# A decoder layer with 32 streamed experts: gathering four experts at once, first weights by column halves, the far branch moved to the end

## The chip, the cores and the metric

The kernel runs on one core of a Trainium2 chip. The metric is the device time of one execution in microseconds (us). Time before: 1111.27 us, the median of three runs (1111.09 to 1114.21).

## The reference, cut to what matters

One post-norm decoder layer on 256 tokens of width 1024, all in float32. After the attention part comes a mixture of 32 experts, of which each token takes four:

```python
x = layer_norm(ALPHA * x + mix, ln1_g, ln1_b)          # after attention
logits = x @ w_router + b_router
top_vals, top_idx = top_k(logits, 4)
gates = softmax(top_vals)
for each expert e, over the tokens that chose it:
    h = x @ w1[e] + b1[e]                               # 1024 -> 2048
    glu = minimum(h[..., 0::2], 7); lin = clip(h[..., 1::2], -7, 7)
    y = (glu * sigmoid(1.702 * glu) * (lin + 1)) @ w2[e] + b2[e]   # 1024 -> 1024
    moe += gate * y
out = layer_norm(ALPHA * x + moe, ln2_g, ln2_b)
```

The weights of all experts are read once: 32 x (8 + 4) MiB.

## The kernel before

**Stages.** Until about 143 us the kernel computes the attention part and the routing. From there on it goes through the 32 experts, one after the other, and ends with the second norm.

**The weight stream.** The list `stream` holds 384 blocks of 1 MiB, twelve for each expert: eight of w1, each 128 rows of all 2048 columns (one row of 8 KB in a partition), and four of w2, each 256 rows of 1024 columns (two rows of 4 KB in a partition). The last four blocks are w2 of expert 31 by column halves (rows of 2 KB, two DMAs a block). SyncE issues them in this order. There are NB = 23 places in on-chip memory (15 in `arena`, 8 named `later`), and block i goes to the place of block i - 23, so its DMA waits until all that reads block i - 23 is done. `load(n)` issues the blocks up to number n; where it stands in the program decides on which reader a block waits. An expert's first twelve places are therefore the last limit of the stream: while expert e - 1 holds its twelve, only blocks up to 12e + 10 are out.

**One expert on TensorE.** The class `Ordered` and the dictionary `last` keep each engine's instructions in the order in which the program writes them. For each expert TensorE does: four bias matmuls (`first_biases`, `ph<-b_s,sel`), 32 matmuls of the first product into the two halves of `ph` (for each of eight row blocks k both halves n, 64 token slots times two column groups side by side), the clamped SwiGLU on VectorE and ScalarE (`swiglu`), four transposes of its result (`turn_act`), 16 matmuls of the second product (`second`), and at every even expert the matmuls that add the pair before to the sums (`combine`). At every odd expert the next two experts' tokens are gathered (class `Pair`): four 128x512 matmuls with token rows as the result, a copy, eight transposes, eight scaled copies into `XG`. This work fills the wait for the SwiGLU.

**More than 64 tokens.** Experts 4 to 29 (`INLINE`) have a branch for 32 further slots (`more`), taken if the expert's count is above 64. In this data one expert takes it, expert 4. It stands behind the first matmul of the next expert, and only after it are the twelve places of the expert free (`load(e * NW + NB)` behind it). For experts 4 to 9 (`TWICE`) it is in two parts: `more_first` in the expert itself, after its first product, which frees the eight w1 places, and `more_second` in the next expert. All that is left (more than 64 tokens in experts 0 to 3, 30, 31, or more than 96) is in one far branch at expert `HOST` = 20, on TensorE, VectorE, ScalarE and SyncE, never taken here. Branches that are expected to be skipped have a hint on TensorE (`expect`); the far branch has none.

**Norm rows.** The residual ALPHA * (normed x * g + b) is added at experts 21 to 28 (`KEPT`), in eight pieces: `spread_cols` makes rows of g and b on TensorE (four 128x128 matmuls each), VectorE makes the piece, one matmul with the identity adds it. g2 and be2 of the second norm are made in the same way at expert 30.

Of the kernel before, what the change touches and what calls it, by code (L numbers as in the profile page):

```python
# [20 lines left out]
P = 128  # L21
# [23 lines left out]
TWICE = range(4, 10)  # L45
HOST = 20
KEPT = 21
MORE = ((64, 32), (96, 32), (128, 64), (192, 64))
@with_exitstack
def decoder_layer(ctx, tc, x, w_in, b_in, sinks, w_out, b_out, ln1_g, ln1_b, w_router, b_router,  # L50
# [26 lines left out]
    MW = 6016  # L77
# [350 lines left out]
    wl = w2[0, NE - 1].rearrange("(a m i p) f -> m p a i f", a=2, m=2, p=P)  # L428
# [184 lines left out]
    XG = V(M, KD, 2 * SLOTS)  # L613
    XTOK = V(M + 1024, 2, 512)
    OH = V(M + 2048, NT, 2 * SLOTS)
    GOH = V(M + 2304, NT, 192)
    GSB = [V(M + 2688 + i * S, S) for i in range(2)]
    Y = [V(M + 3200 + i * 512, 512) for i in range(2)]
    GLU, LIN, AT = (M + 4224 + i * 512 for i in range(3))
    KEEP = V(M + 5760, 2, P)  # L620
    xnT = V(M + 1024, KD, P)
    rt = GLU
    b2_sb = V(M + 3200, D)[0:NE]
    gT = V(M + 2688, S)[0:NE]
# [87 lines left out]
    class Pair:  # L712


        def __init__(self, e, px):
            self.e, self.px = e, px

        def choose(self, t):
            for i in range(2):
                chosen(OH[:, t, i * SLOTS:(i + 1) * SLOTS], self.e + i, t, 0, SLOTS)  # L720

        def tokens(self, t, ns=(0, 1)):
            for n in ns:
                pe.matmul(self.px[n], OH[:, t, :], xn[:, t, n * 512:(n + 1) * 512],
                          start=(t == 0), stop=(t == NT - 1))

        def copy(self):
            act.copy(XTOK[:, 0, :], self.px[0])
            dve.tensor_copy(XTOK[:, 1, :], self.px[1])

        def turn(self, pts):
            pts = [pt.rearrange("p (a b) -> p a b", a=4) for pt in pts]
            for n in range(2):
                for i in range(4):
                    pe.transpose(pts[n][:, i, :], XTOK[:, n, i * P:(i + 1) * P], ident)
            for i in range(4):
                for n in range(2):
                    affine(XG[:, n * 4 + i, :], pts[n][:, i, :], n * 4 + i, n)

# [4 lines left out]
    def first_biases(hs, e):  # L744
        for n in range(2):
            for j in range(2):
                first_bias(hs[n][j * 64:(j + 1) * 64, :], e, SLOTS, j * 1024 + n * 512)

    first = Pair(0, banks[2:4])
# [31 lines left out]
    first.tokens(0, (0,))  # L781
    norm(1, 0)
    route(1)
    first.tokens(0, (1,))
    first_biases([ph[:, n, :] for n in range(2)], 0)
# [3 lines left out]
    first.tokens(1)  # L789
    first.copy()  # L790
    first.turn(banks[0:2])
# [4 lines left out]
    def gather(e, off, w):  # L796
# [3 lines left out]
        xg, xtok = V(M + 1024, KD, SLOTS), V(M + 1024, D)[:, :wq]  # L800
# [25 lines left out]
    def turn_act(aT, i0, n, lin):  # L826

        pa = TP().rearrange("p (a b) -> p a b", a=4)
        for i in range(n):
            pe.transpose(pa[:, i, :], V(lin + i * P, P), ident)  # L830
        act.copy(aT[:, i0:i0 + n, :], pa[:, :n, :])

    def second(w2s, aT, swap=0, label=None):

        py = TP()
        for k in range(KD):
            if k == 2 and label:
                expect(label)
            for j in range(2):
                n = j ^ swap  # L840
                pe.matmul(py[j * 64:(j + 1) * 64, :], aT[:, k % 4, k // 4 * 64:(k // 4 + 1) * 64],
                          w2s[k // 2][:, k % 2, n * 512:(n + 1) * 512], start=(k == 0), stop=(k == KD - 1))
        return py
# [45 lines left out]
    def last_second(w2s, hs):  # L889

        aT = V(AT, 4, P)
        ys, py = (Y[1], V(GLU, 512)), (TP(), ph[:, 1, :])

# [5 lines left out]
        def turn(m):  # L899
            pa = ph[:, 1 - m, :].rearrange("p (a b) -> p a b", a=4)  # L900
            for i in range(2):
                pe.transpose(pa[:, i, :], V(LIN + m * 256 + i * P, P), ident)
            act.copy(aT[:, 2 * m:2 * m + 2, :], pa[:, :2, :])

# [4 lines left out]
        for m in range(2):  # L909
            swiglu(hs[m], 256, GLU + m * 256, LIN + m * 256, AT + m * 256)  # L910
            if m == 0:
                turn(0)
        step(0, 0, 0)
        turn(1)
        act.activation(small[:, 255:256], small[:, 255:256], AF.Sqrt)
        step(0, 0, 1)
# [12 lines left out]
    def over_first(e, b, w1v, xg, lin):  # L929
# [4 lines left out]
        for n in range(wq // 512):  # L934
# [3 lines left out]
            for k in range(KD):  # L938
                for j in range(nq):
                    c0 = j * wq + n * 512  # L940
                    pe.matmul(po[j * w:(j + 1) * w, :], xg[:, k, :w], w1v[k][:, c0:c0 + 512],
                              start=False, stop=(k == KD - 1))
            swiglu(po, 256, GLU + n * 256, lin + n * 256, M + 1536 + n * 256)
# [36 lines left out]
    def expect(label):  # L980

        with tc.issue_after(last[pe].ins):
            tc.mark_branch_hint_location(label, "LikelyTaken", [EN.PE])
# [8 lines left out]
    def more(e, c, w1s, w2s, b=0, deep=False, label=None):  # L992

        off, w = MORE[b]
        with behind(c, off, label):
            w1v = w1s() if callable(w1s) else w1s
            xg = gather(e, off, w)
            over_weights(e, b)
            n = over_first(e, b, w1v, xg, LIN)
            gsb = over_rows(b)  # L1000
            aT = V(M + 1536, 4, P)
            turn_act(aT, 0, n, LIN)
# [3 lines left out]

    def more_first(e, c, w1s):

        with behind(c, MORE[0][0], f"first{e}"):
            n = over_first(e, 0, w1s, gather(e, *MORE[0]), GLU + 256)  # L1010
            turn_act(KEEP, 0, n, GLU + 256)

    def more_second(e, c, w2s):

# [92 lines left out]
    for e in range(NE):  # L1107
# [5 lines left out]
        if e == NE - 1:  # L1113
            hs[1] = TP()
            TP.places = [TP()]
# [182 lines left out]
```

## Time and profile before

| | before |
|---|---|
| median of three runs | 1111.27 us |
| the profiled execution | 1111.0 us |
| its span in the trace | 1109.3 us |
| mean granted clock of TensorE | 0.989 |
| bytes moved | 423.70 MB, mean 382 GB/s |
| TensorE busy | 1039.1 us (94%) |
| VectorE, ScalarE busy | 283.9 us, 181.8 us |
| SyncE's DMA queue | 94.6% of sixteen engines' span |

The page divides the span into 40 slices of 27.7 us; a TensorE that waits for weights inside a run of pipelined matmuls still counts as busy there, so the bytes per slice say more than the busy share. The views by stretch give the mean rate of all DMA traffic in a stretch (last column). 1 MiB is 1.0486 MB, so at r GB/s a block takes 1048.6 / r us.

### The profile page before, as it was taken

How to read it: one execution, taken by the hardware profiler on the slowest of the kernel's cores; microseconds unless marked ns; L12 is line 12 of the kernel's file. 1: busy time of each engine (PE TensorE's matmuls, PEld its weight loads, DVE VectorE, ACT ScalarE, POOL GpSimd, SP SyncE). 2: the span in 40 equal slices, each digit the busy share in tenths (PEclk: the TensorE clock that was granted, in tenths of full speed). 3: DMA queues.
4: the chain of work that ended last, by engine and by line, in shares of the span. 5: the costliest groups of instructions: out<-in, count | busy, mean ns of one | idle time of the engine just before them, and what ended most of it. 6: DMA issues, size and time to landing. Idle time of an engine off the chain costs nothing. (4 is left out here: it accounts for less than half of the span.)

```text
span 1109.3 us, 11948 instructions
## 1 busy us (share of the span) xinstructions
PE 1039.1 (94%) x4634; PEld 417.4 (38%) x4634; DVE 283.9 (26%) x687; ACT 181.8 (16%) x374; POOL 7.1 (1%) x20
## 2 busy tenths in 40 slices
PE   8789899999899999999999999979999999899995
PEld 7465433333233333333333333323333333333431
DVE  6666532121221212121212121211222121221114
ACT  5434421011010101010101010100101010011102
POOL 0000000000000000000000000000000000000001
PEclk9999999999999999999999999999999999899998
DMA  9978599998978999999999999989999999999993
GB/s 331 283 296 328 222 371 416 417 417 326 409 299 347 417 415 417 408 419 417 418 417 417 416 417 414 416 326 387 416 417 417 415 416 416 416 416 415 417 413 121
DMA packets 85952, 423.70 MB, mean 382 GB/s; under 512 B 8256, under 2 KB 15200, under 8 KB 52992
## 3 DMA queue, kind: packets, MB, share of 16 engines
q1 hardware_dynamic: 85568, 422.02, 94.6%
q8 instruction: 65, 1.06, 0.4%
q10 hardware_dynamic: 288, 0.36, 0.1%
q14 instruction: 31, 0.25, 0.1%
HBM read 421.30 MB, written 1.05 MB: 381 GB/s over the span
## 5 line engine op out<-in xcount | busy, mean ns | idle before, releaser
L127 PE MATMUL ph<-arena 128*64 128x512 f32 (+3 forms) x1424 | 340.1, 585 | 7.5 <-DVE small L127 2.6
L127 PE MATMUL bank<-arena 128*64 128x512 f32 (+7 forms) x976 | 261.3, 578 | 11.6 <-DVE arena L127 5.2
L127 PE MATMUL ph<-later,arena 128*64 128x512 f32 x688 | 171.2, 604 | 16.9 <-PEq L988 14.7
L127 PEld LDWEIGHTS ph<-arena 128*64 128x64 f32 (+2 forms) x1424 | 110.7, 139 | 194.9 <-issue 174.5
L127 PEld LDWEIGHTS bank<-arena 128*64 128x64 f32 (+4 forms) x976 | 87.4, 147 | 155.4 <-issue 131.7
L127 DVE TENSOR_SCALAR arena<-ph 128x512 f32<-128x512 f32 (+1 forms) x64 | 40.7, 677 | 402.3 <-PE ph L127 303.1
L127 ACT COPY arena<-bank 128x512 f32<-128x512 f32 (+5 forms) x143 | 70.9, 508 | 425.3 <-PE bank L127 229.4
L127 PE MATMUL bank<-later,arena 128*64 128x512 f32 (+1 forms) x456 | 99.3, 595 | 0.3 <-PEq L988 0.3
L127 PEld LDWEIGHTS ph<-later,arena 128*64 128x64 f32 x688 | 55.8, 139 | 113.3 <-issue 108.1
L127 DVE COPY arena<-bank 64x512 f32<-64x512 f32 (+2 forms) x57 | 38.0, 667 | 218.3 <-PE bank L127 218.3
L127 ACT ACTIVATE arena<-arena 128x512 f32<-128x512 f32 (+1 forms) x34 | 20.8, 611 | 400.8 <-DVE arena L127 400.8
L127 PE MATMUL bank<-early,early 128*128 128x512 f32 (+1 forms) x240 | 57.8, 395 | 5.0 <-ACT early L127 5.0
L127 PE MATMUL bank<-x_sb,arena 128*128 128x512 f32 (+1 forms) x144 | 60.7, 582 | 0.8 <-DVE arena L127 0.8
L127 PE MATMUL bank<-ident,arena 128*128 128x128 f32 x279 | 45.1, 284 | 12.2 <-DVE arena L127 9.2
L127 PEld LDWEIGHTS bank<-later,arena 128*64 128x64 f32 (+1 forms) x456 | 29.9, 133 | 58.7 <-issue 55.0
L127 PEld LDWEIGHTS bank<-ident,arena 128*128 128x128 f32 x279 | 30.1, 140 | 56.6 <-DVE arena L127 24.9
L127 PEld LDWEIGHTS bank<-early,early 128*128 128x128 f32 x240 | 43.3, 203 | 15.3 <-ACT early L127 5.0
L127 DVE TENSOR_TENSOR arena<-arena 128x512 f32<-128x512 f32 (+3 forms) x66 | 36.5, 575 | 3.8
L127 PEld LDWEIGHTS bank<-x_sb,arena 128*128 128x128 f32 (+1 forms) x144 | 23.3, 181 | 36.5 <-issue 35.9
L127 DVE TENSOR_SCALAR arena<-ph,cols 128x128 f32<-128x128 f32 x60 | 24.6, 409 | 45.1 <-ACT arena L127 45.1
L127 ACT ACTIVATE arena<-ph,cols 128x128 f32<-128x128 f32 x60 | 27.5, 458 | 26.9 <-DVE arena L127 21.6
L127 DVE TENSOR_TENSOR early<-arena,early 128x1024 fp32r<-128x1024 f32 (+1 forms) x24 | 24.9, 1046 | 20.0 <-ACT early L127 19.8
(106 smaller groups left out, 314.6 us busy)
## 6 DMA issues: line engine op xcount, KB each, us to landing
arena<-in_w_dram SPq DMA_DIRECT2D x244, 1024.0 KB, 19.2
later<-in_w_dram SPq DMA_DIRECT2D x136, 1024.0 KB, 19.8
arena<-in_w_in_dram SPq DMA_DIRECT2D x10, 512.0 KB, 10.6
arena<-in_w_dram SPq DMA_DIRECT2D x8, 512.0 KB, 14.3
arena<-in_w_in_dram SPq DMA_DIRECT2D x3, 1024.0 KB, 9.7
arena<-in_w_out_dram SPq DMA_DIRECT2D x4, 512.0 KB
arena<-in_w_out_dram SPq DMA_DIRECT2D x2, 1024.0 KB
arena<-in_xt_dram SPq DMA_DIRECT2D x4, 256.0 KB, 3.8
```

What stands on the lines that cost most here:

```text
L127: ins = getattr(self.engine, name)(*a, **k)
```

## The change

- **Gather.** The class `Group` takes four experts at a time, with features on partitions at once: for each of eight feature blocks, `xn` is the stationary operand and the 256 slots of four experts are the columns (16 matmuls of 128x256), and a scaled copy puts the result into `XG`. No token rows, no transposes. It is done once in four experts (e % 4 == 3), in the middle of `second`.
- **First weights by column halves.** A w1 block is now 256 rows of 1024 columns (two rows of 4 KB in a partition). The first product runs over half n = 0 (four blocks), then n = 1; SwiGLU of a half runs beside the next half or the second product. The bias matmuls come two for each half.
- **One check for each expert.** `TWICE`, `more_first` and `more_second` are gone; the branch is whole, behind the first matmul of the next expert, for all of `INLINE`.
- **The far branch** moves from expert 20 to the start of expert 31, behind all the loads on SyncE, with hints on TensorE, VectorE and ScalarE.
- **Norm rows.** At experts 10, 12, 14 and 16 ScalarE issues two DMAs each (`fetch_rows`: 128 partitions, 1 KB of a row, the same for all), and both residual pieces are made from them; `spread_cols` is gone. g2 and be2 come by two DMAs of 512 KB on SyncE behind the last weight block.
- The order of rows in the last expert's w2 blocks and of the slots in `second` is adapted to the halves.

```diff
 LATE = (0, 1, 2, 3, NE - 2, NE - 1)
 INLINE = range(4, NE - 2)
-TWICE = range(4, 10)
-HOST = 20
-KEPT = 21
+KEPT = (10, 12, 14, 16)
...
     for e in range(NE):
-        stream += [w1[0, e, k * P:(k + 1) * P, :] for k in range(KD)]
+        stream += [w1[0, e, k * 256:(k + 1) * 256, n * FF:(n + 1) * FF].rearrange("(k p) f -> p k f", p=P)
+                   for n in range(2) for k in range(4)]
...
-    class Pair:
+    class Group:
...
+        def rows(self, t, r):
+
             for i in range(2):
...
+                k = 2 * r + i
+                pe.matmul(self.places[r][:, i * 256:(i + 1) * 256], xn[:, t, k * P:(k + 1) * P], OH[:, t, :],
+                          start=(t + i == 0), stop=(t + i == NT))
+
+        def copy(self, r):
+            for i in range(2):
+                affine(XG[:, 2 * r + i, :], self.places[r][:, i * 256:(i + 1) * 256], 2 * r + i, i)
...
+    def fetch_rows(q):
+
+        for i, src in enumerate((ln1_g, ln1_b)):
+            act.dma_start(out=ROWS[:, i, :], in_=src[0:1, q * 256:(q + 1) * 256].to_broadcast([P, S]))
...
     for e in range(NE):
+        if e == NE - 1:
+
+            last.clear()
+            with tc.If(count(NE, CENG + [EN.SP]) > MORE[0][0], preferred_fallthrough_block=True, label="late"):
...
+        aT = V(AT, 4, P)
+        for n in range(2):
+            if e or n:
+                first_biases(ph[:, n, :], e, n)
+            for k in range(KD):
+                for j in range(2):
+                    pe.matmul(ph[j * 64:(j + 1) * 64, n, :], XG[:, k, q * SLOTS:(q + 1) * SLOTS],
+                              w1s[n * 4 + k // 2][:, k % 2, j * 512:(j + 1) * 512],
+                              start=False, stop=(k == KD - 1))
...
+                if at == (0, 0) and e and inline(e - 1):
+                    more(e - 1, c, wt[(e - 1) * NW:(e - 1) * NW + KD], wt[(e - 1) * NW + KD:e * NW],
+                         label=f"second{e - 1}")
+                    load(e * NW + NB)
+                    if e in KEPT:
+                        fetch_rows(KEPT.index(e))
...
+                if at == (1, 5):
+                    turn_act(aT, 2, LIN, ph[:, 0, :])
+            swiglu(ph[:, n, :], 256, GLU + n * 256, LIN + n * 256, AT + n * 256)
...
+        py = banks[4 + odd]
+        second(py, w2s, aT, range(3), odd)
+        turn_act(aT, 2, LIN, ph[:, 0, :], 2)
...
+        second(py, w2s, aT, range(3, 4), odd)
...
+        elif q == 3:
+            for r in range(4):
                 for t in range(NT):
-                    nxt.tokens(t)
...
+                    nxt.rows(t, r)
+                nxt.copy(r)
+        second(py, w2s, aT, range(4, KD), odd)
...
+        if e == NE - 2:
+            for i, src in enumerate((ln2_g, ln2_b)):
+                spread((g2, be2)[i], src)
```

Three places in the order of instructions (`ph` is the tile of the first product, `bank_93` and `bank_94` are the two banks of the second product and of the small work, `x_sb` holds the normed tokens, `later_...` and `arena` the weights or small tiles). TensorE at the end of expert 3, before: the last part of the first product, the gather of experts 4 and 5, the transposes of the SwiGLU result (`bank_94<-ident`), the transposes of the gather (`ph<-ident`), the second product.

```order
L127 MATMUL ph<-arena 64x512 x20
L127 MATMUL bank_94<-x_sb,arena 128x512
L127 MATMUL bank_93<-x_sb,arena 128x512
L127 MATMUL bank_94<-x_sb,arena 128x512
L127 MATMUL bank_93<-x_sb,arena 128x512
L127 MATMUL bank_94<-ident,arena 128x128 x4
L127 MATMUL ph<-ident,arena 128x128 x8
L127 MATMUL bank_93<-arena 64x512 x12
L127 MATMUL bank_93<-later_567,arena 64x512 x4
```

The same place in the changed kernel: second half of the first product with two transposes of the first half's SwiGLU inside it, the first six matmuls of the second product, the other two transposes, then the gather of experts 4 to 7.

```order
L125 MATMUL ph<-arena 64x512 x12
L125 MATMUL ph<-ident,arena 128x128 x2
L125 MATMUL ph<-arena 64x512 x4
L125 MATMUL bank_94<-arena 64x512 x6
L125 MATMUL ph<-ident,arena 128x128 x2
L125 MATMUL bank_94<-arena 64x512 x2
L125 MATMUL ph<-arena,x_sb 128x256 x16
L125 MATMUL bank_94<-arena 64x512 x4
L125 MATMUL bank_94<-later_567,arena 64x512 x4
```

The gather moved from between the two products into the second one, and its transposes are gone. TensorE in expert 5, before: its own check (`COMPARE_AND_BRANCH`, the branch `more_first`) stands behind its first product, after three rows of it.

```order
L127 MATMUL ph<-arena 64x512 x4
L1293 BRANCH_PREFETCH_HINT
L127 MATMUL ph<-arena 64x512 x12
L1023 TENSOR_LOAD cnt
L1023 ISA x2
L988 COMPARE_AND_BRANCH
L127 MATMUL bank_94<-x_sb,arena 32x256 x8
```

The changed kernel, from the second product of expert 5 to the first matmul of expert 6: the only check of expert 5.

```order
L125 MATMUL bank_94<-arena 64x512 x2
L125 MATMUL bank_94<-later_567,arena 64x512 x4
L125 MATMUL bank_94<-later_569,arena 64x512 x4
L990 TENSOR_LOAD cnt
L990 ISA x2
L125 LDWEIGHTS sel_67
L125 MATMUL ph<-b_s,sel_67 64x512
L125 LDWEIGHTS sel_67
L125 MATMUL ph<-b_s,sel_67 64x512
L125 MATMUL ph<-arena 64x512
L968 COMPARE_AND_BRANCH
```

The w1 places of an expert from 4 to 9 now stay held until the next expert has begun. SyncE at the far branch, before: it stands between the loads of expert 20 and the rest, and its last instruction waits for all eight DMA semaphores.

```order
L145 DMA arena<-in_w_dram 128x2x1024 [waits DMAHW6_49]
L145 DMA arena<-in_w_dram 128x2x1024 [waits DMAHW7_49,PE_49]
L1023 TENSOR_LOAD cnt [waits DVE_49]
L1137 COMPARE_AND_BRANCH
L1137 UNCONDITIONAL_BRANCH [waits SP_sequencer_49,DMAHW0_49,DMAHW1_49,DMAHW2_49,DMAHW3_49,DMAHW4_49,DMAHW5_49,DMAHW6_49,DMAHW7_49]
```

The changed kernel: the branch comes behind the last weight DMAs (512 columns each) and the two norm rows.

```order
L149 DMA arena<-in_w_dram 128x2x512 [waits DMAHW7_49,PE_49]
L149 DMA arena<-in_w_dram 128x2x512 [waits DMAHW0_49,PE_49]
L169 DMA arena<-in_ln_g_dram 128x1024 [waits DMAHW1_49,PE_49]
L169 DMA arena<-in_ln_b_dram 128x1024 [waits DMAHW2_49,PE_49]
L990 TENSOR_LOAD cnt [waits DVE_49]
L1076 COMPARE_AND_BRANCH
```

No weight load stands behind SyncE's far branch any more.

## Rows read from the trace of the kernel before

**Rows 1.** The page: 40 slices of the span; clock in tenths, then GB/s.
```profile
PEclk9999999999999999999999999999999999899998
GB/s 331 283 296 328 222 371 416 417 417 326 409 299 347 417 415 417 408 419 417 418 417 417 416 417 414 416 326 387 416 417 417 415 416 416 416 416 415 417 413 121
```

**Rows 2.** Stretches (PE, PEld, DVE, ACT, POOL busy; PEclk, DMA share, GB/s): rates.
```profile
360.00:740.00 380.00, 364.44 (x1574) 135.52 (x1574) 70.11 (x148) 44.81 (x88) 0.00 (x0) 1.00 1.02 416
844.00:864.00 20.00, 19.85 (x94) 7.88 (x92) 2.76 (x6) 1.56 (x4) 0.00 (x0) 1.00 1.02 420
864.00:874.00 10.00, 9.35 (x38) 3.12 (x34) 2.67 (x4) 1.22 (x2) 0.00 (x0) 1.00 1.02 409
1078.00:1086.00 8.00, 6.55 (x32) 1.89 (x28) 2.58 (x7) 0.89 (x3) 0.00 (x0) 1.00 1.01 375
24.00:30.00 6.00, 6.00 (x29) 4.91 (x28) 5.93 (x10) 2.55 (x5) 0.00 (x0) 1.00 1.11 365
```

**Rows 3.** The same view: stretches with pauses of the stream, and its end.
```profile
268.00:272.00 4.00, 2.34 (x27) 0.99 (x30) 0.96 (x4) 1.63 (x6) 0.00 (x0) 1.00 0.15 59
308.00:312.00 4.00, 3.84 (x20) 1.18 (x18) 0.00 (x0) 0.00 (x0) 0.00 (x0) 1.00 0.02 4
740.00:760.00 20.00, 15.79 (x59) 5.72 (x56) 3.05 (x5) 1.22 (x2) 0.00 (x0) 0.91 0.65 256
940.00:960.00 20.00, 15.86 (x62) 5.64 (x60) 3.22 (x11) 1.23 (x3) 0.00 (x0) 0.83 1.01 415
1088.00:1090.00 2.00, 2.00 (x12) 0.62 (x10) 0.00 (x0) 1.31 (x2) 0.00 (x0) 1.00 0.29 106
```

**Rows 4.** Waits of SyncE's queue: line, waited for, total us, times, longest.
```profile
SPq L1137 <- SPq L1137: 19.1, 8, 2.5
```

**Rows 5.** Timeline of SyncE: start, us, DMAs that it issued after the pauses.
```profile
272.72 0.37 SPq L145 DMA_DIRECT2D later<-in_w_dram  x1
...
311.68 2.51 SPq L145 DMA_DIRECT2D arena<-in_w_dram  x5
...
346.50 1.45 SPq L145 DMA_DIRECT2D arena<-in_w_dram  x3
```

**Rows 6.** Timeline of TensorE: first matmul of expert 0, then experts 2 to 4.
```profile
143.75 1.94 PE L127 MATMUL ph<-arena 128*64 128x512 f32 x8
...
196.92 0.60 PE L127 MATMUL ph<-b_s,sel 96*64 96x512 bf16 x4
...
222.54 0.60 PE L127 MATMUL ph<-b_s,sel 96*64 96x512 bf16 x4
...
237.54 3.70 PE L127 MATMUL bank<-x_sb,arena 128*128 128x512 f32 x8
...
241.56 1.13 PE L127 MATMUL ph<-ident,arena 128*128 128x128 f32 x8
...
249.53 0.60 PE L127 MATMUL ph<-b_s,sel 96*64 96x512 bf16 x4
```

**Rows 7.** The same, where expert 4 takes its branch, in two parts.
```profile
268.24 1.07 PE L127 MATMUL bank<-x_sb,arena 128*32 128x256 f32 x16
...
280.98 3.66 PE L127 MATMUL bank<-later,arena 128*64 128x512 f32 x16
...
289.54 0.87 PE L127 MATMUL bank<-ident,arena 128*128 128x128 f32 x4 [0.19 <-ACT arena L127]
...
298.58 0.65 PE L127 MATMUL ph<-arena 128*64 128x512 f32 x2
```

**Rows 8.** Groups of instructions: busy us, mean ns of one | idle before.
```profile
L127 PE MATMUL bank<-arena,ident 128*128 128x256 f32 x16 | 5.6, 431 | 0.0
```

**Rows 9.** The chain of work that ended last, from TensorE's last matmuls.
```profile
1093.75 1.89 PE ph L127 x8
1095.67 0.59 ACT arena L127
1096.31 1.14 PE bank L127 x2
```

**Rows 10.** Timeline of TensorE at a skipped branch of expert 26.
```profile
946.28 2.79 PE L127 MATMUL ph<-later,arena 128*64 128x512 f32 x5 [4.14 <-PEq L988]
```

More of the change, by code (lines that the diff above doesn't have):

```diff
@@ L780, in decoder_layer @@
     logits(1, 1)
-    first.tokens(0, (0,))
+    first.rows(0, 0)
+    first.rows(0, 1)
     norm(1, 0)
     route(1)
-    first.tokens(0, (1,))
-    first_biases([ph[:, n, :] for n in range(2)], 0)
+    first.rows(0, 2)
+    first.rows(0, 3)
     ranks(1)
@@ L788, in decoder_layer @@
     norm(1, 1)
-    first.tokens(1)
-    first.copy()
-    first.turn(banks[0:2])
+    first_biases(ph[:, 0, :], 0, 0)
+    for r in range(4):
+        first.rows(1, r)
+        first.copy(r)
     acc = [[banks[2 * t + n] for n in range(2)] for t in range(NT)]
@@ L824, in swiglu, with turn_act, second @@
         dve.tensor_tensor(lin, lin, sg, op=ALU.mult)
[L826 to L829 removed]
+    def turn_act(aT, n, lin, pa=None, i0=0):
+        pa = (TP() if pa is None else pa).rearrange("p (a b) -> p a b", a=4)
+        for i in range(i0, i0 + n):
             pe.transpose(pa[:, i, :], V(lin + i * P, P), ident)
[L831 to L838, printed above, removed]
+        act.copy(aT[:, i0:i0 + n, :], pa[:, i0:i0 + n, :])
+    def second(py, w2s, aT, ks, swap=0):
+        for k in ks:
             for j in range(2):
                 n = j ^ swap
[L841 removed]
+                pe.matmul(py[j * 64:(j + 1) * 64, :], aT[:, k // 4 * 2 + k % 2, k // 2 % 2 * 64:(k // 2 % 2 + 1) * 64],
                           w2s[k // 2][:, k % 2, n * 512:(n + 1) * 512], start=(k == 0), stop=(k == KD - 1))
[L843 removed]
     def weighted(dst, e, t, off, w):
@@ L1005, in more @@
                 more(e, c, w1s, w2s, b + 1, deep)
[L1007 to L1013, printed above, removed]
-        with behind(c, MORE[0][0], f"second{e}"):
-            over_weights(e, 0)
-            over_second(0, w2s, KEEP, over_rows(0))
     CENG = [EN.PE, EN.DVE, EN.Activation]
@@ L1104, in late @@
         more(e, count(e, CENG + [EN.SP]), get(0, KD), get(KD, 4), b, True)
-    g2, be2 = xn[:, 0, :], xn[:, 1, :]
+    g2, be2 = (view(block(spare[6]), 2, D)[:, i, :] for i in range(2))
     for e in range(NE):
+        if e == NE - 1:
+            last.clear()
+            with tc.If(count(NE, CENG + [EN.SP]) > MORE[0][0], preferred_fallthrough_block=True, label="late"):
+                for f in LATE:
+                    late(f)
+                for f in INLINE:
+                    late(f, 1)
+                last.clear()
@@ new lines, in decoder_layer @@
+        w2s = wt[e * NW + KD:(e + 1) * NW]
+        if e == NE - 1:
+            last_second(w2s, aT)
+            break
+        py = banks[4 + odd]
+        second(py, w2s, aT, range(3), odd)
+        turn_act(aT, 2, LIN, ph[:, 0, :], 2)
+        label = f"second{e}" if inline(e) else "late" if e == NE - 2 else None
+        if label:
+            expect(label)
+        if label == "late":
+            expect(label, dve)
+            expect(label, act)
+        second(py, w2s, aT, range(3, 4), odd)
@@ L1195, in decoder_layer @@
+        if odd == 0:
+            for t in range(NT):
+                for n in range(2):
+                    (start_sums if e == 0 else combine)(t, n)
+        elif q == 3:
+            for r in range(4):
+                for t in range(NT):
+                    nxt.rows(t, r)
+                nxt.copy(r)
+        second(py, w2s, aT, range(4, KD), odd)
         for j, copy in enumerate((dve.tensor_copy, act.copy)):
```

218 lines of the change are left out of this document (64 added, 154 removed).

## The prediction

> **What bounds the kernel now.** I read the slices of the page first [rows 1]. From slice 14 on (360 us) the rate is 413 to 419 GB/s in all but three of them, and the stretch 360 to 740 us has a mean of 416 [rows 2]. TensorE seems 90% busy there too, but two of its experts show what it needs by itself: expert 2 took 222.54 - 196.92 = 25.62 us and expert 3 took 249.53 - 222.54 = 26.99 us [rows 6], while twelve blocks at 416 GB/s take 12 x 2.52 = 30.2 us. So after 360 us the weight stream sets the time and TensorE waits inside its runs. Before that it is the other way: slices 9, 11 and 12 have 326, 299 and 347 GB/s [rows 1], because the stream had no free place. The fine stretches show the pauses: 59 GB/s from 268 to 272 us, 4 from 308 to 312 [rows 3], and SyncE's next DMAs at 272.72, 311.68 and 346.50 us [rows 5]. These are the moments at which expert 4 freed its w1 places (inside its overflow branch), expert 5 and expert 6 theirs (behind their first checks). The third pause ends at 346.50 with the block that takes the place of expert 6's first: block 6 x 12 + 23 = 95. From there on the stream runs to its end but for one hole: slice 26 (740 to 760 us: 256 GB/s [rows 3]), where SyncE at the far branch waits for its outstanding DMAs, eight waits of up to 2.5 us [rows 4], before it issues the next. The traffic ends inside 1088 to 1090 us (106 GB/s there [rows 3]), at about 1088.7.
>
> So the time is: the moment at which the stream runs for good, plus the blocks left times their price, plus holes, plus the tail. Check on the kernel before: blocks 95 to 383 are 289, the last four of them in rows of 2 KB. An 8 KB block costs 1048.6/420 = 2.497 us, a 4 KB block 1048.6/409 = 2.564, one of 2 KB rows 1048.6/375 = 2.796 [rows 2]. With eight of the first kind to four of the second a block is 2.519 us. From 347.2 (0.7 us after the issue): 285 x 2.519 = 717.9, 4 x 2.796 = 11.2, hole 20 x (1 - 256/416) = 7.7, which gives 1084.0. It is 4.7 us short, that is 0.016 us a block; I add that to each block below.
>
> **The change part by part.**
>
> *Gather and order of an expert.* An odd expert without a gather loses the 3.70 and 1.13 us of it [rows 6]: 26.99 - 4.83 = 22.2 us. Every fourth expert has 16 matmuls of 256 columns; the nearest row is 0.431 us for one [rows 8], so 6.9 us and an expert of 29.1. The SwiGLU of a half lies beside 16 matmuls or the first six of the second product, so I let it cost nothing; if that cover fails it is about a microsecond an expert. Four experts: 25.6 + 22.2 + 25.6 + 29.1 = 102.5 us, before 2 x (25.62 + 26.99) = 105.2. Before expert 0, four experts' slots are made instead of two; no row shows this, I take 1.2 us later (0 to 3). After 360 us all this is beside the stream and worth nothing.
>
> *One check instead of two, experts 4 to 9.* This moves the pauses. Expert 0 starts at 143.75 + 1.2 = 144.95 instead of 143.75; before, the first product of expert 4 began 0.44 after 249.53, that is 106.2 after expert 0's, 1.0 more than the two pairs; now 144.95 + 102.5 + 1.0 = 248.5, its biases at 248.0 and those of expert 5 at 273.6. There the whole overflow of expert 4 stands behind the first matmul. Its two parts were 280.98 - 268.24 = 12.7 and 298.58 - 289.54 = 9.0 us [rows 7], together 21.8. Expert 6 begins at 273.6 + 22.2 + 21.8 = 317.6. With the stream the same story: 71 blocks are allowed until expert 4's places come free, in about 271 us they have landed; expert 4's twelve come free from about 281 us and last until about 312; expert 5's come free only at expert 6's check, 1.5 us into it and some 0.7 for a branch, at 319.9. The stream restarts for good at about T = 320.6, with block 5 x 12 + 23 = 83. Before, block 95 at 347.2; now at that time (347.2 - 320.6)/2.58 = 10.3 blocks more, block 93.3. The position is 1.7 blocks or 4.4 us behind. Later checks cost nothing: TensorE has 25 us of work to 31 of stream. What is queued behind the check is SyncE's next load, and with eleven blocks out (28 us) it isn't late. T has bounds of 3 us on either side from the start of expert 0 and the uncovered SwiGLU.
>
> *First weights by column halves.* A row of 8 KB in a partition becomes two of 4 KB, as w2 has now. w2 stretches show 409 GB/s beside 420 in w1 stretches [rows 2], so all blocks now cost 2.564 + 0.016 = 2.580 us. Of the 301 blocks left at T, 297 have 4 KB rows: 766.3 us; the last four 11.2. Against a price of 2.519 + 0.016 that is 297 x 0.045 = 13.4 us more. The Trainium skill ("DMA: Bandwidth & Descriptors", Why small descriptors are slow) gives three cycles a packet beside one for each 32 bytes; by that an 8 KB row costs 259 cycles and two of 4 KB cost 262, 1.2% and not the 2.7% of the rows, and the term would be about 6 us. The rows are of the same queue and win; the rule is inside the range.
>
> *The far branch.* The hole of 7.7 us goes: no load stands behind it on SyncE. TensorE, VectorE and ScalarE meet it at the start of expert 31. TensorE's stall at a skipped branch was 4.14 us at its worst [rows 10], and TensorE has 12 x 0.45 = 5 us of slack in the twelve blocks that follow, so I take nothing; 0 to 5 us for the range.
>
> *Norm rows.* Eight small fetches write 8 x 128 KB = 1.05 MB in 1 KB rows; at 365 GB/s, the stretch of 1 KB rows [rows 2], that is 2.9 us, with their starts 3.0. They share the eight DMA semaphores with SyncE, and ScalarE waits in `fetch_rows` for a DMA that is long done; if it weren't, SyncE's next block would wait for ScalarE. Bounds 2.5 to 5 (twice 2.5). g2 and be2 are 1 MB behind the last block, 2.6 us, and are used about 4 us after the last matmul: hidden by the statistics. The matmuls of `spread_cols` go (16 of 256 columns and more), but TensorE waits for the stream there: nothing.
>
> *The tail.* Before, TensorE was late: the traffic ended at 1088.7, its last matmuls at 1095.64, the copy behind them at 1095.67 [rows 9], and from there to the span's end are 1109.3 - 1095.67 = 13.6 us, which the change leaves alone. The lateness came from work at experts 27 and 30 (a 4.14 us stall at clock 0.83 [rows 3, 10], `spread_cols` for the norm) that is gone or moved. Now TensorE should be at the last block: 0.5 to 1.9 us from its landing to the last matmul, so a tail of 14.1 to 15.5, I take 15.0, against 20.6.
>
> *Sum.* 320.6 + 766.3 + 11.2 + 3.0 = 1101.1; + 15.0 = 1116.1 span; the profiled execution before had 1111.0 - 1109.3 = 1.7 outside its span, so 1117.8, I say 1117.8 us. This profiled execution is 0.3 us under the median, which I neglect. In differences to before: position +4.4, row size +13.4, hole -7.7, fetches +3.0, tail -5.6; about +7 us.
>
> **The rivals.**
>
> *Half rows cost nothing (faster).* The difference of 409 to 420 may belong to w2's stretches and not to the row size: each w2 block is one contiguous megabyte, and the places differ. Then the 8 blocks in 12 that are w1 (8 x 25 = 200 from T on) keep 2.497: 200 x 0.067 = 13.4 us less, 1104.4 us, 0.6% faster than before. It decides if w1's price stays under about 2.52. For it: nothing in the queue changes but the row. Against it: rows of 2 KB and 1 KB are slower still in order (375, 365). By the Trainium skill (the same page, Rules for kernel authors), 128 partitions and at least 1 MiB a DMA give the full bandwidth, which both forms satisfy. The trace disagrees, with 409 against 420. Chance 0.14.
>
> *Places come free early.* If the skipped checks hold the w1 places less than I think, or TensorE reaches expert 6 some 9 us sooner, the second pause goes and T is about 312: 1109 us, no difference. For it: before, the places were freed by the matmul that read them last. Against it: the order puts the branch, which reads all twelve, in the next expert. Chance 0.08.
>
> *A new stall.* ScalarE's fetches wait and hold back SyncE, at four places, or TensorE stands at the last branch and comes out at the low clock level, as at 940 to 960 us (granted 0.83 [rows 3]). One hole of 5 us each at four places is 1117.8 + 20 = 1138; the stall at the end alone, 4 us and as much again at half the clock, less the slack of 5, is 1121. Chance 0.17.
>
> **How the numbers follow.** A measurement of this kernel tells about 0.3% from no change: faster is under 1108, slower over 1114.6. The forecast has 0.61; its own spread (T by 3, the price of rows between the rule's and the rows', the fetches) reaches from 1111 to 1123, and a fifth of it lies under 1114.6. Faster: 0.14 and a little, 0.15. Same: 0.08 + 0.12 = 0.20. Slower: 0.48 + 0.17 = 0.65. The range takes in the free half rows below and half of the new stalls above: 1104 to 1130.
>
> **What would show it.** Stretches of w1 loads after 360 us at 409 GB/s and not 420 (the row term, on which the sign hangs); two pauses, at about 271 to 281 and 312 to 320 us, and none after; no slice under 400 GB/s after slice 12; TensorE's expert of 22 us where the gather was; traffic ending near 1101 and the span 15 us later. The prediction is wrong if w1 stretches show 415 or more, if a third pause stands where rows are fetched, or if the tail is still 20 us.

## The result and the profile after

The changed kernel takes 1169.08 us (median of four runs, 1165.25 to 1171.50), against 1112.32 for the kernel before beside it: a ratio of 1.0506 with a 95% interval of 1.0468 to 1.0543. The forecast was 1117.8. The direction was right, the size was not: 56.8 us instead of about 7.

The page of the changed kernel, the lines that answer to [rows 1] (40 slices of 29.1 us; clock in tenths, GB/s):

```profile
PEclk9899999999999999999999999999999999999988
GB/s 332 263 305 298 269 340 409 409 409 168 296 237 410 359 399 369 401 409 367 409 359 410 395 386 408 409 409 409 409 409 409 409 408 408 409 408 408 408 390 95
```

Two things are to be seen. The plateau is at 408 to 409 GB/s, where it was 416 to 417. And before slice 24 it is a plateau only in places: 168, 296 and 237 in slices 9 to 11, and seven further slices under 400.

The stretches behind these slices (busy of PE, PEld, DVE, ACT, POOL; PEclk, DMA share, GB/s), to be set beside [rows 2, 3]:

```profile
276.00:292.00 16.00, 15.41 (x72) 5.05 (x70) 2.67 (x7) 1.78 (x5) 0.00 (x0) 1.00 0.00 1
332.00:340.00 8.00, 8.00 (x38) 2.40 (x34) 2.04 (x5) 1.00 (x3) 0.00 (x0) 1.00 0.01 4
404.00:408.00 4.00, 3.85 (x18) 1.28 (x16) 0.68 (x1) 0.58 (x1) 0.00 (x0) 1.00 0.22 45
462.00:466.00 4.00, 4.00 (x22) 1.76 (x20) 0.00 (x0) 0.00 (x0) 0.00 (x0) 1.00 0.58 131
780.00:1060.00 280.00, 252.33 (x1066) 91.65 (x1064) 46.20 (x122) 26.52 (x61) 0.00 (x0) 0.99 1.03 408
1120.00:1124.00 4.00, 1.29 (x6) 0.94 (x8) 1.11 (x4) 0.10 (x1) 0.00 (x0) 0.59 1.00 392
1124.00:1128.00 4.00, 4.00 (x10) 0.79 (x10) 0.00 (x0) 0.55 (x2) 0.00 (x0) 0.56 1.03 385
1142.00:1144.00 2.00, 1.80 (x10) 0.49 (x6) 1.47 (x4) 0.42 (x1) 0.00 (x0) 1.00 0.15 61
```

There are two pauses, as forecast, but they come later and last longer: from about 275 to 297 us and from about 331 to 341 (forecast 271 to 281 and 312 to 320). The first two stretches lie inside them and have next to no traffic for 16 and 8 us. Further holes follow. The two pauses end when expert 4's overflow and expert 6's check free places, so the question is why TensorE came there late. Its timeline at the start of expert 1, at the gather of experts 4 to 7 and through experts 4 to 6 says it (start us, us, operation, in brackets the idle time before and what ended it; a float32 matmul is two records there, so four times x8 are the 16 matmuls of the gather):

```profile
173.93 0.39 PE L125 MATMUL ph<-b_s,sel 96*64 96x512 bf16 x2
...
247.03 1.99 PE L125 MATMUL ph<-arena,x_sb 128*128 128x256 f32 x8
250.26 1.99 PE L125 MATMUL ph<-arena,x_sb 128*128 128x256 f32 x8 [1.24 <-DVE arena L125]
253.49 1.99 PE L125 MATMUL ph<-arena,x_sb 128*128 128x256 f32 x8 [1.24 <-DVE arena L125]
256.72 1.99 PE L125 MATMUL ph<-arena,x_sb 128*128 128x256 f32 x8 [1.24 <-DVE arena L125]
258.64 1.94 PE L125 MATMUL bank<-arena 128*64 128x512 f32 x8
...
262.12 0.39 PE L125 MATMUL ph<-b_s,sel 96*64 96x512 bf16 x2
...
270.24 0.41 PE L125 MATMUL ph<-b_s,sel 96*64 96x512 bf16 x2 [0.85 <-DVE arena L125]
...
289.56 0.39 PE L125 MATMUL ph<-b_s,sel 96*64 96x512 bf16 x2
...
338.86 0.39 PE L125 MATMUL ph<-b_s,sel 96*64 96x512 bf16 x2
```

The gather takes 258.64 - 247.03 = 11.6 us, with a wait for VectorE ahead of each pass but the first; 6.9 were forecast. And the bias matmuls of an expert's second half wait 0.85 us for VectorE (0.86 to 0.93 in experts 0 to 3), which reads the first half. Expert 4 begins at 262.12 (forecast 248.0) and expert 6 at 338.86 (forecast 317.6). TensorE's list of waits sums them up (total us, times, longest):

```profile
PE ph L125 <- DVE arena L125: 55.6, 55, 1.2
...
PE ph L125 <- ACT arena L125: 15.0, 33, 0.5
```

At the end, expert 31, VectorE and TensorE behind the far branch (L1076 is that branch), and the chain that ends last:

```profile
1115.06 2.75 PE L125 MATMUL ph<-arena 128*64 128x512 f32 x12
...
1122.22 1.11 DVE L125 TENSOR_SCALAR arena<-iota,rank,gates 128x128 f32<-128x128 f32 x4 [6.47 <-PEq L1076]
1122.71 1.15 PE L125 MATMUL bank<-ident,arena 128*128 128x128 f32 x4 [4.90 <-DVE arena L125]
```
```profile
1144.57 7.46 PE bank L125 x28
1152.05 0.59 ACT arena L125
```

TensorE passes the branch, does six matmuls (12 records) and then waits 4.90 us for the gate rows that VectorE makes, since VectorE stood 6.47 us at the branch. Its granted clock is 0.59 in the stretch 1120 to 1124 above, in which this wait ends, and 0.56 in 1124 to 1128, close to the lower of its two levels (1.2 and 2.4 GHz). At the end it is still late: the traffic has nearly stopped at 1144 us, and 14 matmuls in a row (28 records) follow before the copy at 1152.05. This copy comes 13.4 us before the end, where [rows 9] had 13.6.

### The profile page after: what moved, and what is told of

Its sections match the earlier page's. It is cut to its first block, busy times and chain, and to the rows that moved or that the text cites. A ratio compares the mean times of both kernels' runs of the same rounds, so it can differ in the third digit from the quotient of the medians.

```text
span 1165.5 us, 11836 instructions
## 1 busy us (share of the span) xinstructions
PE 1035.2 (89%) x4538; PEld 415.1 (36%) x4538; DVE 280.4 (24%) x763; ACT 170.2 (15%) x384; POOL 7.1 (1%) x20
## 2 busy tenths in 40 slices
DMA packets 120160, 425.79 MB, mean 365 GB/s; under 512 B 8416, under 2 KB 16384, under 8 KB 119968
## 3 DMA queue, kind: packets, MB, share of 16 engines
q8 instruction: 64, 1.05, 0.4%
HBM read 423.40 MB, written 1.05 MB: 364 GB/s over the span
## 5 line engine op out<-in xcount | busy, mean ns | idle before, releaser
L125 PE MATMUL bank<-arena 128*64 128x512 f32 (+6 forms) x984 | 268.8, 583 | 6.9 <-DVE arena L125 4.7
L125 DVE TENSOR_SCALAR arena<-ph 128x256 f32<-128x256 f32 x128 | 48.3, 419 | 473.6 <-PE ph L125 372.2
L125 PEld LDWEIGHTS bank<-arena 128*64 128x64 f32 (+3 forms) x984 | 87.6, 147 | 157.2 <-issue 140.0
L125 ACT COPY arena<-bank 128x256 f32<-128x256 f32 (+4 forms) x97 | 43.9, 470 | 314.2 <-DVE arena L125 203.3
L125 PE MATMUL ph<-arena,x_sb 128*128 128x256 f32 x232 | 58.0, 392 | 25.9 <-DVE arena L125 25.9
L125 ACT ACTIVATE arena<-arena 128x256 f32<-128x256 f32 x65 | 27.1, 416 | 297.3 <-DVE arena L125 288.1
L125 ACT COPY arena<-ph 128x256 f32<-128x256 f32 (+1 forms) x65 | 24.1, 370 | 251.8 <-PE ph L125 251.8
L125 PEld LDWEIGHTS ph<-arena,x_sb 128*128 128x128 f32 x232 | 41.7, 189 | 44.5 <-DVE arena L125 34.4
L125 PE MATMUL ph<-b_s,sel 96*64 96x512 bf16 x128 | 25.4, 386 | 29.1 <-DVE arena L125 29.1
L125 DVE TENSOR_TENSOR arena<-arena 128x256 f32<-128x256 f32 (+4 forms) x101 | 45.8, 469 | 7.5 <-DVE arena L125 0.5
L125 PE MATMUL bank<-ident,arena 128*128 128x128 f32 x147 | 24.4, 289 | 11.6 <-DVE arena L125 10.0
## 6 DMA issues: line engine op xcount, KB each, us to landing
arena<-in_w_dram SPq DMA_DIRECT2D x8, 512.0 KB, 14.1
```

The lines of the kernel that those rows point to most:

```text
L125: ins = getattr(self.engine, name)(*a, **k)
```

## The experiments

Times of before in the comparisons are those of runs on the same chip beside the kernel (1112.8 to 1114.7). Differences between two variants of the changed kernel are those of their medians, mostly of two runs each and not all from one chip; the medians of before differ by up to 1.9 us between these occasions, so such a difference is known to some 2 us.

**The row size alone.** The kernel before, w1 blocks by column halves:

```diff
-        stream += [w1[0, e, k * P:(k + 1) * P, :] for k in range(KD)]
+        stream += [w1[0, e, k * 256:(k + 1) * 256, n * FF:(n + 1) * FF].rearrange("(k p) f -> p k f", p=P)
+                   for k in range(4) for n in range(2)]
...
-            if not inline(e):
+            if not inline(e) and k % 2:
                 load(e * NW + k + 1 + NB)
```

> The kernel before with w1 blocks of 256 rows by 1024 columns (two rows of 4 KB in a partition), the two column halves of a row block one behind the other; for the experts outside the branch two blocks are issued after every second row block, so that none is overwritten before it is read (in before_half_rows it was, so that kernel says nothing of the row size). If half rows cost what w2's stretches say, 190 w1 blocks at 0.066 us more give 12.6 us: about 1125, and no stretch above 411 GB/s. If half rows are free: 1112.

Measured: 1130.17 against 1114.74, a ratio of 1.0131 (1.0090 to 1.0173), 14.6 us by the ratio. The stretch 780 to 1060 us of this kernel, where that of before has 416 GB/s:

```profile
780.00:1060.00 280.00, 272.72 (x1152) 105.64 (x1149) 56.07 (x122) 31.45 (x62) 0.00 (x0) 1.00 1.03 409
```

Half rows cost about what w2's stretches said, 14.6 us for the 12.6 expected. (A first form, before_half_rows, without the second edit took 1338.1 us; its loads came over rows not yet read, and it tells nothing of the row size.)

**The row size the other way.** The kernel before, w2 with one row of 8 KB in a partition:

```diff
-        stream += [w2[0, e, k * 256:(k + 1) * 256, :].rearrange("(k p) f -> p k f", p=P)
+        stream += [w2[0, e, k * 256:(k + 1) * 256, :].rearrange("(p k) f -> p (k f)", k=2)
...
+        lv = V(lin, n * P).rearrange("p (c f k) -> p c k f", f=P, k=2)
...
-            pe.transpose(pa[:, i, :], V(lin + i * P, P), ident)
+            pe.transpose(pa[:, i, :], lv[:, i // 2, i % 2, :], ident)
```

> The row size turned the other way: the kernel before with w2 rows 2p and 2p + 1 in partition p, one row of 8 KB instead of two of 4 KB that are 128 rows apart (the transposes of the SwiGLU result take every second column, so the product is the same). If the price hangs on the bytes in a row, w2 stretches rise from 409 to 420 GB/s and 95 w2 blocks after the third pause cost 0.067 us less each: 6.4 us, about 1108. If w2's lower rate has another cause, no difference: 1114.

Two stretches, a long one and the one that was w2 alone in the kernel before (409 in [rows 2]):

```profile
780.00:1060.00 280.00, 274.82 (x1194) 104.62 (x1192) 57.21 (x120) 34.36 (x66) 0.00 (x0) 0.99 1.01 420
864.00:874.00 10.00, 9.86 (x39) 3.63 (x36) 2.67 (x4) 0.82 (x2) 0.00 (x0) 1.00 1.02 423
```

The rate does what was expected, 423 for 409. The time doesn't quite: 1111.31 against 1113.20, a ratio of 0.9976 (0.9954 to 0.9998), 2.7 us where 6.4 were expected, and 6.4 lies outside the interval. Why the rest is missing is not settled.

**One check alone.** The kernel before with one line changed:

```diff
-TWICE = range(4, 10)
+TWICE = ()
```

> The kernel before with one check for each expert (TWICE empty), all else as before. The stream then restarts for good at expert 6's check, about 328 us, with block 83, where before it stood at block 95 at 347.2, that is at block 83 at 316.8: 11 us later, about 1123. If the time of the release doesn't matter, because TensorE's path is the same and the stream catches up, 1112.

1124.30 against 1114.74, 1.0079 (1.0043 to 1.0114), some 9 us. The second pause is now some 15 us long (one stretch of this kernel):

```profile
319.00:334.00 15.00, 14.85 (x69) 5.88 (x69) 4.74 (x9) 4.05 (x8) 0.00 (x0) 1.00 0.11 25
```

So the late release was a real cost, and it has about the size of the argument (11 us expected); the forecast had counted on the shorter experts to make up for part of it.

**The far branch's hole.** The kernel before without its far branch (not taken here):

```diff
-                if e == HOST:
-                    last.clear()
-                    with tc.If(count(NE, CENG + [EN.SP])
-                               > MORE[0][0], preferred_fallthrough_block=False):
...
```

> The kernel before without its far branch (which these inputs don't take). The hole of 7.7 us at 740 to 760 us goes; if the stream alone sets the time, 1104 to 1105. If TensorE, which before is some 5 us late at the end, takes part of it, 1108.

1108.09 against 1114.74, 0.9934 (0.9912 to 0.9956): 7 us. The stretch that had 256 GB/s in [rows 3]:

```profile
740.00:760.00 20.00, 19.74 (x82) 6.98 (x78) 3.36 (x5) 1.80 (x3) 0.00 (x0) 1.00 1.02 415
```

**The fetches of norm rows.** The changed kernel, the same eight DMAs from GpSimd:

```diff
-            act.dma_start(out=ROWS[:, i, :], in_=src[0:1, q * 256:(q + 1) * 256].to_broadcast([P, S]))
+            pool.dma_start(out=ROWS[:, i, :], in_=src[0:1, q * 256:(q + 1) * 256].to_broadcast([P, S]))
```

> The changed kernel with the eight norm-row fetches issued by GpSimd instead of ScalarE, so that they share no semaphore with the weight DMAs of SyncE; same bytes. If the four holes at experts 10, 12, 14 and 16 (3.4, 3.1, 3.3 and 2.6 us of traffic, 12.4 together) come from SyncE waiting for a fetch that ScalarE issues late, they vanish: about 1157 us, at best; less is won where TensorE is late at these places and the stream then stops for want of free places. If they come from the fetches' bytes or from places that come free late, they stay: 1169.

1166.40 (two runs, 1164.67 to 1168.13), a median inside the range of the changed kernel's own runs. SyncE's wait in the changed kernel, and two stretches of this one (the first is the hole at expert 10, the second lies where expert 14 begins):

```profile
SPq L143 <- DMA arena<-in_ln_g_dram: 58.1, 4, 15.5
```
```profile
462.00:466.00 4.00, 3.85 (x18) 1.24 (x15) 0.68 (x1) 0.58 (x1) 0.71 (x1) 1.00 1.03 405
566.00:578.00 12.00, 8.94 (x40) 2.91 (x37) 2.32 (x7) 1.30 (x4) 0.00 (x0) 1.00 0.88 325
```

The four waits are real, 58.1 us of them, and the hole at expert 10 closes without them; but later holes open instead (325 GB/s above). A miss. In the changed kernel ScalarE issues the fetch of expert 10 at 460.99 us, right behind a copy that waited 4.80 us for VectorE, which had waited 5.57 us for TensorE: ScalarE is late there because TensorE is.

**Three result places for the gather.** The changed kernel:

```diff
-                    nxt = Group(e + 1, [ph[:, r % 2 ^ 1, :] for r in range(4)])
+                    nxt = Group(e + 1, [ph[:, 1, :], ph[:, 0, :], banks[4], ph[:, 1, :]])
```

> The changed kernel with three result places for the gather of four experts (both halves of ph and bank 4) instead of two. In the changed kernel each of the four passes of a gather takes 3.23 us, 1.24 of it waiting until its place is copied out. If that wait is what makes the gather long, a gather takes 9.2 instead of 12.9 us, the stream starts for good 3.7 us sooner and TensorE's four experts fall from 116.6 to 112.9 us: about 1160 to 1165. If the passes are long for another reason, 1169 and passes of 3.23.

1156.41 (two runs), 12.7 us less, more than the 3.7 us of the one gather before the pauses: the later, shorter gathers count too. So TensorE, not the stream alone, set the time far beyond the second pause.

**ph as two tiles.** The changed kernel with one declaration changed, two tiles of a bank each behind the same indices:

```diff
-    ph = pmem.tile([P, 2, 512], F32, name="ph")
+    class Halves:
+        def __init__(self):
+            self.tiles = [pmem.tile([P, 512], F32, name=f"ph{n}") for n in range(2)]
+        def __getitem__(self, at):
+            return self.tiles[at[1]][at[0], at[2]]
+    ph = Halves()
```

> The changed kernel with ph as two tiles of one bank each instead of one tile of two banks; nothing else. In the changed kernel the bias matmuls of the second half wait 0.92 us for VectorE's two reads of the first half, and each pass of a gather waits 1.24 us for the copies of the pass before, though these are in the other bank. If the waits come from ph being one tile for the ordering of reads and writes, they go: TensorE's waits on VectorE at ph fall from 55.6 us to under 15, four experts from 116.6 to about 110 us, the stream starts for good 7 us sooner and some of the later holes close: about 1150. If the waits are the hardware's, 1169.

1137.06 (two runs, 1135.66 to 1138.45): 32.0 us less, more than half of the whole loss, from no change in work. The timeline at the start of expert 1, at the same gather and through expert 4's halves, then the first rows of TensorE's list of waits. The row of 55.6 us for `ph` on VectorE's tiles in `arena` is gone from it, and the one on ScalarE is down from 15.0 to 0.3 us:

```profile
173.68 0.39 PE L134 MATMUL ph<-b_s,sel 96*64 96x512 bf16 x2
...
241.84 7.17 PE L134 MATMUL ph<-arena,x_sb 128*128 128x256 f32 x32
...
252.43 0.39 PE L134 MATMUL ph<-b_s,sel 96*64 96x512 bf16 x2
...
259.52 0.39 PE L134 MATMUL ph<-b_s,sel 96*64 96x512 bf16 x2
```
```profile
PE ph L134 <- PEq L977: 28.3, 9, 5.2
PE bank L134 <- DVE arena L134: 14.8, 9, 4.9
```

The gather is one run of 7.17 us (6.9 were forecast), the second half starts without a wait, expert 4 at 252.43 instead of 262.12. From expert 1's start to expert 4's are 252.43 - 173.68 = 78.75 us, before this edit 262.12 - 173.93 = 88.19. The waits came from the ordering of reads and writes, which took the two banks as one object, not from the hardware. The holes at the row fetches close by themselves but for some 2 us at expert 10, though SyncE still waits 34 us there: it has a lead to wait from. On this kernel's page only two slices between 12 and 37 are under 400 GB/s (381 and 398).

**Far branch at expert 31.** Left out of the changed kernel, and of the kernel with two tiles:

```diff
-            with tc.If(count(NE, CENG + [EN.SP]) > MORE[0][0], preferred_fallthrough_block=True, label="late"):
-                for f in LATE:
-                    late(f)
...
```

> The changed kernel without the far branch (which these inputs don't take): what it costs at expert 31 all engines. If the 6.5 us in which VectorE stands at this branch and the low clock that follows make TensorE late at the end, the tail from the last landing to the end falls from 24.7 to about 15 us: 1159. If TensorE is late at the end because its experts are too long, it stays near 1167.

1160.86 (1160.44 to 1161.28), 8.2 us less.

> The changed kernel with ph as two tiles and without the far branch. Beside after_two_tiles (1137) it shows the price of the branch at expert 31 where the rest is mended. If VectorE's stand at the branch and the low clock behind it make the late end, 8 us less as in after_no_far: 1129. If the stream's end covers it there, 1137.

1130.24 (1127.88 to 1132.61), 6.8 us less than with two tiles alone. The branch at the end costs about as much as the hole that it avoids. The DMA queues of the changed kernel from 1118 to 1122 us, inside VectorE's stand at the branch (packets, MB, share of time), have two rows beside that of the weights:

```profile
q8 instruction: 1, 0.02, 1.7%
q14 instruction: 2, 0.02, 1.3%
```

So instructions are loaded during the stand. In after_no_far there is no such packet from 1100 to 1120 us, where expert 31 begins (at 1115.31), and one in 1120 to 1122; in before_far_at_end four lie from 1056 to 1061 us, in the stand shown below. Whether these loads are what holds the engines no run tests.

**The checks of experts 5 to 9**, left out beside two tiles:

```diff
-                    more(e - 1, c, wt[(e - 1) * NW:(e - 1) * NW + KD], wt[(e - 1) * NW + KD:e * NW],
+                    if e - 1 not in range(5, 10):
+                      more(e - 1, c, wt[(e - 1) * NW:(e - 1) * NW + KD], wt[(e - 1) * NW + KD:e * NW],
                          label=f"second{e - 1}")
```

> The changed kernel with ph as two tiles and without the branches of experts 5 to 9 (which these inputs don't take); expert 4's stays. Their twelve places then come free with the last matmul that reads each. If the one check for each expert is what holds the places, the second pause (8.9 us of traffic at 318 to 333) goes: 1128. If TensorE's path to expert 6 sets it, the pause stays: 1137.

1127.71 (1127.02 to 1128.40), 9.4 us less. The second pause, in after_two_tiles and here:

```profile
318.00:333.00 15.00, 14.85 (x70) 5.52 (x68) 1.61 (x4) 0.95 (x2) 0.00 (x0) 1.00 0.50 168
```
```profile
318.00:333.00 15.00, 15.00 (x74) 5.02 (x72) 2.66 (x6) 1.40 (x4) 0.00 (x0) 1.00 1.03 409
```

**All three mended** (two tiles, no far branch, no checks of 5 to 9):

> The changed kernel with ph as two tiles, without the far branch and without the branches of experts 5 to 9 (none of them taken here). If the prices found one by one add up, 1137 - 7 - 9.4 = 1121; what is then left over the kernel before without its far branch (1108) should be the half rows, 13 to 15 us. If they hide each other, 1126.

1121.39 (1120.12 to 1122.84). The prices add up. Over before_no_far (1108.09) that leaves 13.3 us by the medians, and 17 by the two ratios to before (1.0087 and 0.9934); the half rows' 14.6 lies between.

**Two tiles and GpSimd's fetches:**

> The changed kernel with ph as two tiles and the norm rows fetched by GpSimd. SyncE still waits 34 us at the fetches in after_two_tiles, but the stream shows one hole of 1.5 us there. If the fetches cost only where TensorE is late, nothing is won: 1135 to 1137. If they have a price of their own, 1130.

1135.91 (1134.68 to 1137.15) for 1137.06: the fetches have no price of their own that shows.

**The far branch elsewhere.** The kernel before with `HOST = 6` and a hint:

> The kernel before with its far branch at expert 6 instead of 20, with a hint on TensorE. There SyncE waits for its outstanding DMAs at a time at which the stream is short of places anyway (the third pause, 343 to 349 us). If the hole at expert 20 is what the far branch costs, it is hidden: about 1107, as without the branch (1108). If TensorE, which sets the pace up to there, loses its time at the branch instead (a stall of 3 to 4 us), 1111 to 1112.

1119.60 against 1113.20, 1.0049 (1.0026 to 1.0072): slower, a miss. The pause it was to hide in grew, and another came (259 and 420 GB/s in the same stretches of before):

```profile
340.00:352.00 12.00, 11.70 (x48) 4.46 (x45) 2.67 (x4) 0.63 (x1) 0.00 (x0) 1.00 0.19 63
480.00:490.00 10.00, 9.85 (x48) 3.36 (x46) 2.38 (x9) 0.58 (x1) 0.00 (x0) 1.00 0.39 138
```

So a load that is held back there is not absorbed; how much of the second hole follows from the first was not tried.

**A version that beats both.** The kernel before with paired w2 rows, the far branch at expert 31, g2 and be2 by DMA, and the last gate rows two row blocks later:

```diff
-            if k == 2 and e == NE - 1:
+            if k == 4 and e == NE - 1:
                 rows_of_last()
-            if k in (3, 4) and e == NE - 1:
-                combine_first(k - 3)
+            if k in (5, 6) and e == NE - 1:
+                combine_first(k - 5)
```

> The kernel before with paired w2 rows (one row of 8 KB), the far branch at the start of expert 31 behind all loads with hints on three engines, g2 and be2 by two DMAs behind the last weight block as in the changed kernel, and the gate rows of the last pair two row blocks later, so that TensorE needn't wait for VectorE while that stands at the branch. If the late end of the changed kernel comes from TensorE waiting for these rows, the hole of 6.7 us is won without it: 1104 to 1106. If the branch at expert 31 costs as much wherever the rows are made, 1111.

1107.82 against 1112.82, 0.9948 (0.9927 to 0.9970), faster than both kernels. The stretch of the old hole, and TensorE at expert 31:

```profile
740.00:760.00 20.00, 19.66 (x83) 7.35 (x81) 4.40 (x9) 1.80 (x3) 0.00 (x0) 1.00 1.01 420
```
```profile
1061.26 0.64 PE L127 MATMUL bank<-b_s,sel 96*64 96x512 bf16 x2 [6.64 <-ACTq L1113]
```

The hole is gone, but TensorE again stands 6.64 us at expert 31, now ahead of its first recorded matmul there (one of the second pair of bias matmuls; the first pair is missing from the trace), with ScalarE's queue at the branch named as what ended it. VectorE stood 5.77 us at the same branch, until 1061.12. So moving the gate rows didn't remove the stand, and the 1104 to 1106 expected are missed; the theory that TensorE is late only through these rows falls. What at this branch takes an engine some 6 us, with hints, stays open; loads of instructions go with it, as shown above.

## Why the prediction was wrong, point by point

**What bounds the kernel.** Right for the kernel before: the weight stream from 347 us on, and a hole of 7.7 us (measured by taking it away: 7). It was carried over to the changed kernel without asking how much lead TensorE has there, and that was the point. In the terms of the sum: in the profiled execution the stream runs for good from about 341 us (320.6 forecast), the traffic with g2 and be2 ends near 1144 (1101.1 + 2.6), and 21.5 us follow (12.4). That is 21 us lost before the stream runs, some 20 in later holes and 9 at the end.

**Gather and order of an expert: this step failed.** The matmuls take 7.17 us for the 6.9 forecast, once they can run, but that is luck: 0.431 us is the mean of one record, a matmul has two records, and these overlap (7.17 / 16 = 0.448 us for a matmul). But "I let it cost nothing" was said of the SwiGLU of a half, and it does cost: 0.85 to 0.93 us at each second half; and the sum had no wait inside the gather, where each later pass waits 1.24 us. The escape in the text, "about a microsecond an expert", was about the size of the one wait, but no term of the sum, and it held the other not at all. Four experts were forecast at 102.5 us; from 145.79, expert 0's first matmul, to expert 4's at 262.35 went 116.6. Experts 1 to 3 alone took 88.2 for 76.9, and 9.4 of these 11.3 us go with after_two_tiles; the rest of the 14.1, more than half of it in expert 0, no run takes apart. The cause of the 9.4 is named by after_two_tiles: `ph` is one tile for the ordering, so a write to one bank waits for reads of the other. It need not have been a surprise: in the order of instructions with its waits, which can be printed before any run, the bias matmul of the second half carries a wait on VectorE. The text had taken the order without the waits.

**What a microsecond is worth.** "After 360 us all this is beside the stream and worth nothing" failed with it. With experts of 29 us (116.6 / 4) beside twelve blocks of 31, the lead hardly grows, and the waits come back as holes up to slice 23, at later checks and fetches; with two tiles all but two of the slices 12 to 23 are back at 400 or more. 32.0 us hung on the two tiles, of which 262.12 - 252.43 = 9.7 show at expert 4.

**One check.** Forecast together with the gather as 4.4 us behind. Alone it costs 9 us in the kernel before; in the changed one, with two tiles, leaving the checks of experts 5 to 9 out altogether gives 9.4. The mechanism was right; what was to make up for part of it, the shorter experts, did not come.

**First weights by column halves.** Right: 408 GB/s in the plateau, 14.6 us for a term of 13.4. By an estimate from the Trainium skill's three cycles a packet ("DMA: Bandwidth & Descriptors", Why small descriptors are slow) two rows of 4 KB cost 1.2% more than one of 8 KB; the traces, 420 to 409 and back to 423 in the same place when the rows are joined, say near 3%. The rows of the trace were the better price.

**The far branch.** The hole goes, as forecast. "I take nothing" for the branch at expert 31 was wrong: 6.8 to 8.2 us. The row of a stall of 4.14 us was for TensorE alone [rows 10]; here VectorE stood 6.47 us, TensorE waited 4.90 us for it and then ran at a clock of 0.59 and 0.56, and the 5 us of slack that the text counted on did not hide it.

**Norm rows.** The bytes were right (423.70 MB before, 425.79 now: the 1.05 of the fetches and the 1.05 of g2 and be2); the 3.0 us for them no run measures alone. The waits were wrong: "a DMA that is long done" was said of ScalarE's wait, while SyncE's next block waits for a fetch that ScalarE has not yet issued. The rival put 5 us on each; the waits were up to 15.5. They cost nothing that shows where the stream has a lead (1135.91 for 1137.06).

**The tail.** 15.0 us were forecast from the last block to the end. TensorE was late again, mostly for the reason above: the traffic is down to 61 GB/s in the stretch 1142 to 1144 and 21.5 us follow, while without the branch (after_no_far, 41 GB/s in the same stretch) 14.7 us follow. The part from the copy on was right: 13.4 for 13.6.

**The rivals.** Free half rows: no (before_half_rows_2). Places free early: no, later. A new stall: this is the family that happened, at both named places, but TensorE's own waits at `ph`, the largest part, were in no rival.

**The account.** Two tiles 32.0, checks 9.4, far branch at the end 6.8, half rows 14.6, less the hole of 7: 55.8 of the 56.8 us. Each price is known to some 2 us only, so that they close so well is in part luck.

## What to carry to other kernels

When a stage is cut into halves so that one half's work hides behind the other's, look whether the ordering sees two objects: read the waits in the instruction order, not only the order. A stage that is "off the path" is so by a lead; size the lead, and see which waits along the way (checks, shared semaphores, branches) use it up, before a longer stage is priced at nothing. A difference in rate between two kinds of transfers in one trace is a usable price, if the rows differ in the thing that is changed.

## What the runs showed that I had not expected

Joining two rows of 4 KB into one of 8 KB in a partition raises a stretch from 409 to 423 GB/s at the same number of bytes. A branch that isn't taken, with a hint on three engines, held VectorE 6.47 us in the changed kernel and TensorE 6.64 us in before_far_at_end. Packets of instructions lie in both stands; whether they are the cause is open.
